# Six recurrence and output gate slabs in the seven-product scheme, with the operand sums kept through the branch projection and the first gates inside it

## The chip, the cores and the metric

The kernel runs on one core of one Trainium2 chip. The metric is the device time of one execution in microseconds (us), median over runs: 917.94 us for the kernel before (3 runs, 917.94 to 918.06). The profile below is of one further execution.

## The reference

One hybrid decoder block over 16 meta tokens and 512 tokens (T = 528), D = 1024, all in float32. Cut to what matters here:

```python
u = rmsnorm(h, mix_norm_w)
proj = u @ w_in                      # 1024 x 8192
q, k, v, g_ret, lru_in, lru_gate, gate_a, gate_b = split(proj)   # 1024 columns each
...                                  # rotary, chunked retention -> o
y_ret = (silu(g_ret) * o) @ w_branch_ret
c = causal_depthwise_conv(lru_in, conv_w, conv_b)                # 4 taps
r = sigmoid(c @ wa + ba);  i = sigmoid(c @ wx + bx)              # 4 blocks of 256 x 256
a = exp(-8 * r * softplus(-lam))
hs = scan(h -> a_t * h + sqrt(1 - a_t**2) * (i * c)_t)           # linear recurrence over time
y_lru = (gelu(lru_gate) * hs) @ w_branch_lru
h = h + (sigmoid(gate_a) * y_ret + sigmoid(gate_b) * y_lru) @ w_out
u = rmsnorm(h, ffn_norm_w)
g, up = split(u @ w_ffn_in)          # 2 x 2816 columns
h = h + (silu(g) * up) @ w_ffn_out
return rmsnorm(h, final_norm_w)[16:]
```

## The kernel before

Activations lie transposed, channels on the 128 partitions and time along the free axis. Every float32 product is made of three matmuls on rounded halves: an operand is stored as `hi` (a cast on ScalarE, line 291) and `lo` (source minus `hi`, a subtraction on VectorE, line 295), and `block` (lines 363 to 375 with `mm3`) issues hi·hi, hi·lo and lo·hi into one PSUM bank.

The weights `w_in` come as 32 **slabs** of 1024 x 256, four for each of the eight parts of `proj`: 16 to 19 are `lru_in`, 20 to 23 `lru_gate`, 24 to 27 `gate_a`, 28 to 31 `gate_b`. `w_fi` has 22 slabs of the same shape. A slab is four quarters `a11`, `a12`, `a21`, `a22` of 128 x 512, each against the matching quarters `b11` ... `b22` of the operand. A **plain** slab makes eight products of quarters (`plain`, 96 matmuls, 256 wide). A **fast** slab (`fast`, `fast512`, `fast528`) makes seven by the Strassen-Winograd scheme (84 matmuls). It needs sums of the weight quarters `s1` to `s4` (line 261, VectorE), sums of the operand quarters `t1` to `t4` (made once), and recombination: `ws` and `pz` (two copies on ScalarE, one add on VectorE, line 394) after the first two products, `u2` (a copy on ScalarE) after the last, and two adds on VectorE (lines 408 and 409) which read the two PSUM banks and so set them free. The product with `s4` goes into the bank that `pz` is read from, so it stands behind `pz`.

`PLAN` is the order of the mixing half: R (retention projections), A (`gate_a`), I (`lru_in` and its convolution), BR (`w_br`, the branch projection of retention, in two halves of eight k steps), T (the gates of one recurrence block, 48 matmuls of 264, each 6 followed by a sigmoid on ScalarE from PSUM), L (`lru_gate`, followed by gelu), B (`gate_b`, followed by tanh) and BL (`w_bl`). After BR stand `T0 L0 I2 T1 L1 I3 L2 T2 B0 L3 T3 B1 B2 B3 BL`. In that part all of L, I2, I3 and B are plain. The operand sums of `w_in` (t1 to t4) are freed ahead of BR.

`conv` (lines 1072 to 1086) is on VectorE: per half a block one tensor_scalar, three scalar_tensor_tensor, and the split into hi and lo. `recurrence` (lines 1113 to 1156) runs per block as a deferred generator, advanced while matmuls are issued: GpSimd multiplies `g*c` (line 1120, 1056 wide), ScalarE makes exp, tanh and sqrt, VectorE five scalar_tensor_tensor for each half, GpSimd `g1*t` (line 1146, 528 wide), VectorE a scan (line 1148), and at the end the product with the gelu (line 1153). ScalarE loads a function table when the function changes (sigmoid, exp/tanh, sqrt, gelu).

A timeline-driven scheduler puts the instructions of each engine in their final order when the program is built. On the chip each engine then takes its instructions in that order, and a consumer waits by semaphore. PSUM has eight banks, handed out in turn, so the first matmul into a bank waits for the reader that frees it. `pz`, `ws` and `u2` have one buffer each.

After BL come `w_out`, the residual, `out_norm` (norm factors, transposes with a diagonal matrix made on GpSimd for tiles 2 and 3), and the FFN: slabs 0 to 2 of `w_fi` are plain (slabs 0 and 1 by token halves), 3 to 21 fast, then `w_fo`.

Of the kernel before, what the change touches and what calls it, by code (L numbers as in the profile page):

```python
# [153 lines left out]
def hybrid_block(ctx: ExitStack, tc: tile.TileContext, a: dict):  # L154
# [60 lines left out]

    def plain_slab(key, i):
        if key == "w_in":
            return i in [{"Q": Q, "K": K, "G": G}[r[0]] + int(r[1]) for r in PLAIN_R] or LI + 2 <= i < GA or i >= GB
        return key == "w_fi" and i <= FIRST

    pieces = []
    for n, (key, i) in enumerate(order):
# [225 lines left out]
        plain("w_in", s, 256, [(pb[:, :256], pb[:, 256:]) for pb in pbs], UV)  # L448
        return pbs

    def branch(key, source, done):


        parts = {}
        for hf in range(2):
# [22 lines left out]
        nc.gpsimd.tensor_tensor(r[:parts, :w], v[:parts, :w], mhalf[:parts, :w], op=ALU.pow)  # L478
        return r[:parts, :w]

    def rms_factors(src, name, parts=P, diagonal=True):

        scratch = get(D)
        ssq = small.tile([P, 1], F32, tag="ssq", bufs=4, name=f"ssq_{name}")
        nc.scalar.activation(scratch[:parts], src, AF.Square, accum_out=ssq[:parts])
# [584 lines left out]
        convs[b] = defer(conv(b, xp, x3), 0.0)  # L1070

    def conv(b, xp, x3):
        c, ch, cl = get(2 * T), get(2 * T, F32R), get(2 * T, F32R)
        lru[b] = (c, ch, cl)
        c3, ch3, cl3 = (t.rearrange("p (j t) -> p j t", j=2) for t in (c, ch, cl))
        for j in range(2):
            k = 2 * b + j
            cw = [vec[:, V_CW + i * 8 + k:V_CW + i * 8 + k + 1] for i in range(4)]
            nc.vector.tensor_scalar(c3[:, j], x3[:, j], cw[3], vec[:, V_CB + k:V_CB + k + 1], ALU.mult, ALU.add)
            for i in range(1, 4):  # L1080
                nc.vector.scalar_tensor_tensor(c3[:, j, i:], x3[:, j, :T - i], cw[3 - i], c3[:, j, i:],
                                               ALU.mult, ALU.add)
# [31 lines left out]
    def recurrence(group):  # L1114
# [2 lines left out]

        A = {}
        for b, r, g, c in group:
            nc.gpsimd.tensor_tensor(g, g, c, op=ALU.mult)  # L1120
# [17 lines left out]
        for b, r, g, c in group:  # L1138
            for j in range(2):
                a, t, d, g1 = two(A[b])[:, j], two(r)[:, j], ds[b, j], two(g)[:, j]  # L1140
                nc.vector.scalar_tensor_tensor(d, a, 1.0, d, ALU.add, ALU.mult)
# [3 lines left out]
                nc.vector.scalar_tensor_tensor(t, a, 1.0, t, ALU.add, ALU.mult)
                nc.gpsimd.tensor_tensor(g1, g1, t, op=ALU.mult)
                yield STEPS[3]
                nc.vector.tensor_tensor_scan(t, a, g1, 0.0, ALU.mult, ALU.add)
# [4 lines left out]
            (nc.gpsimd if Z_POOL else nc.vector).tensor_tensor(z3, z3, two(r)[:, :, NM:], op=ALU.mult)
# [62 lines left out]

    def out_norm(t):
        if t >= 2:
            diag = held = rms_factors(h_sb[t], f"h{t}")
            rows = h_sb[t]  # L1220
        else:
            diag, rows = None, get(D)
            held = rows
            nc.vector.tensor_scalar_mul(rows, h_sb[t], rms_factors(h_sb[t], f"h{t}", diagonal=False))
        yield NORM
        for c in range(2):
            pb = transposed(rows, diag, c, f"hT{t}_{c}")
# [213 lines left out]
```

## Time and profile before

| | |
|---|---|
| median of the runs | 917.94 us (917.94 to 918.06) |
| the profiled execution: time, span | 918.17 us, 916.4 us |
| granted TensorE clock, mean | 0.997 |
| from 285.3 us: BR | 54.70 us |
| 340.0 to 472.2 us: L, I2, I3, T, B | 132.20 us |
| 472.2 to 516.5 us: BL | 44.30 us |
| 516.5 to 564.6 us: `w_out`, norm | 48.10 us |
| 564.6 to 600 us: `w_fi` slabs 0 to 2 | 35.40 us |
| 600 to 786 us: 19 fast slabs of `w_fi` | 186.00 us |

PE is TensorE, DVE is VectorE, ACT is ScalarE, POOL is GpSimd. A row of a group gives the line, the engine, the operation, the names, the shapes and the count, then busy time and mean ns of one. Instructions that follow one another on an engine overlap at their ends by some hundredth of a us, so a mean is longer than the pitch at which they follow.

### The profile page before, as it was taken

What the parts mean: (1) busy time and instruction counts of PE and PEld (TensorE: products, weight loads), DVE (VectorE), ACT (ScalarE), POOL (GpSimd) and SP (SyncE); (2) the same over time, 40 slices, a digit from 0 to 9 for tenths busy, and PEclk for the clock granted to TensorE, in tenths of its full rate; (3) what the DMA queues carried; (4) which work ended last, traced back from release to release, by engine and by line L of the source; (5) the groups of instructions that cost most, each with busy time, mean ns of one, the idle gap of its engine ahead of it and who ended that gap; (6) DMA issues with size and microseconds to landing.
All of it is one profiled execution on the core that took longest, in us unless ns stands there. A gap on an engine that the chain in (4) does not pass through costs nothing.

```text
span 916.4 us, 16814 instructions
## 1 busy us (share of the span) xinstructions
PE 904.4 (99%) x6572; PEld 854.1 (93%) x6572; DVE 657.7 (72%) x1082; ACT 463.2 (51%) x815; POOL 71.4 (8%) x81
## 2 busy tenths in 40 slices
PE   8999999999999999999999999999999999999996
PEld 7999999999999889999998889999999999888885
DVE  5988978986888738768735428878999998832223
ACT  6654546553556256757733315545555556632213
POOL 3000010000100011211200211000000000000003
PEclk9999999999999999999999999999999999999998
DMA  9323132231134332233342223223333333432202
GB/s 332 106 93 105 34 110 77 92 106 43 62 94 138 108 100 82 79 107 123 119 136 92 95 70 104 81 83 104 102 118 104 103 118 107 144 107 92 81 1 92
DMA packets 49071, 92.59 MB, mean 101 GB/s; under 512 B 5584, under 2 KB 5840, under 8 KB 48992
## 3 DMA queue, kind: packets, MB, share of 16 engines
q1 hardware_dynamic: 47408, 87.55, 29.4%
q10 hardware_dynamic: 1584, 3.97, 1.3%
q8 instruction: 51, 0.84, 0.4%
q14 instruction: 28, 0.23, 0.1%
HBM read 89.40 MB, written 2.10 MB: 100 GB/s over the span
## 4 chain that ended last, share of the span: by engine, by line
PE 79%; DVE 0%; issue 0%; POOLq 0%; POOL 0%; ACT 0%
PE fo L363 4%; PE fo L365 4%; PE fo L364 4%; PE zwf L375 4%; PE zwf L373 4%; PE zwf L374 4%; PE yxf L374 3%; PE yxf L375 3%; PE yxf L373 3%; PE gate L373 2%; PE lg L373 2%; PE lg L375 2%; PE gate L375 2%; PE gate L374 2%; PE lg L374 2%; PE wo L363 2%
## 5 line engine op out<-in xcount | busy, mean ns | idle before, releaser
L291 ACT CAST hi<-raw_w_in 128x512 fp32r<-128x512 f32 x99 | 61.0, 620 | 65.0 <-PE w_br L364 13.9
L295 DVE TENSOR_TENSOR lo<-raw_w_in,hi 128x512 fp32r<-128x512 f32 x99 | 70.4, 718 | 29.8 <-ACT hi L291 29.6
L375 PE MATMUL zwf<-b,lo 128*128 128x256 f32 x304 | 84.9, 279 | 0.0
L374 PE MATMUL zwf<-b,hi 128*128 128x256 f32 x304 | 84.9, 279 | 0.0
L373 PE MATMUL zwf<-b,hi 128*128 128x256 f32 x304 | 84.6, 279 | 0.0
L295 DVE TENSOR_TENSOR lo<-raw_w_fo,hi 128x512 fp32r<-128x512 f32 x44 | 30.1, 689 | 63.0 <-ACT hi L291 63.0
L291 ACT CAST hi<-s_w_fi 128x512 fp32r<-128x512 f32 x76 | 47.2, 622 | 45.5 <-PE zwf L374 36.3
L363 PE MATMUL fo<-hi,b 128*128 128x512 f32 x176 | 69.5, 395 | 0.0
L365 PE MATMUL fo<-hi,b 128*128 128x512 f32 x176 | 69.3, 394 | 0.0
L364 PE MATMUL fo<-lo,b 128*128 128x512 f32 x176 | 69.1, 392 | 0.0
L374 PE MATMUL yxf<-b,hi 128*128 128x256 f32 x228 | 63.2, 280 | 0.0
L375 PE MATMUL yxf<-b,lo 128*128 128x256 f32 x228 | 63.0, 279 | 0.0
L291 ACT CAST hi<-raw_w_fo 128x512 fp32r<-128x512 f32 x44 | 27.3, 621 | 69.8 <-PE fo L365 64.2
L291 ACT CAST hi<-raw_w_fi 128x512 fp32r<-128x512 f32 x69 | 42.3, 622 | 39.1 <-PE yxf L374 17.4
L373 PE MATMUL yxf<-b,hi 128*128 128x256 f32 x228 | 61.2, 279 | 0.0
L295 DVE TENSOR_TENSOR lo<-s_w_fi,hi 128x512 fp32r<-128x512 f32 x76 | 52.0, 687 | 12.2 <-ACT hi L291 10.4
L375 PEld LDWEIGHTS zwf<-b,lo 128*128 128x128 f32 x304 | 57.2, 188 | 0.0
L374 PEld LDWEIGHTS zwf<-b,hi 128*128 128x128 f32 x304 | 57.1, 188 | 0.0
L373 PEld LDWEIGHTS zwf<-b,hi 128*128 128x128 f32 x304 | 57.1, 188 | 0.0
L291 ACT CAST hi<-s_w_in 128x512 fp32r<-128x512 f32 x52 | 32.3, 620 | 40.4 <-PE zwgate L374 9.2
L295 DVE TENSOR_TENSOR lo<-raw_w_fi,hi 128x512 fp32r<-128x512 f32 x69 | 47.0, 687 | 6.0 <-ACT hi L291 5.9
L295 DVE TENSOR_TENSOR lo<-s_w_in,hi 128x512 fp32r<-128x512 f32 x52 | 35.5, 687 | 11.3 <-ACT hi L291 11.1
(422 smaller groups left out, 3134.0 us busy)
## 6 DMA issues: line engine op xcount, KB each, us to landing
raw_w_in<-in_w_in SPq DMA_DIRECT2D x112, 256.0 KB, 3.1
raw_w_fi<-in_w_fi SPq DMA_DIRECT2D x88, 256.0 KB, 3.2
raw_w_fo<-in_w_fo SPq DMA_DIRECT2D x44, 256.0 KB, 3.0
raw_w_br<-in_w_br SPq DMA_DIRECT2D x16, 256.0 KB, 3.1
raw_w_bl<-in_w_bl SPq DMA_DIRECT2D x16, 256.0 KB, 3.1
raw_w_out<-in_w_out SPq DMA_DIRECT2D x16, 256.0 KB, 2.9
raw_w_v<-in_w_v SPq DMA_DIRECT2D x15, 256.0 KB, 3.5
b<-in_x SPq DMA_DIRECT2D x4, 512.0 KB, 6.8
```

The lines of the kernel that those rows point to most:

```text
L291: nc.scalar.copy(hi, src)
L295: engine.tensor_tensor(lo, src, hi.bitcast(F32), op=ALU.subtract)
L363: nc.tensor.matmul(out, wh, xh, start=start, stop=False, skip_group_check=True)
L364: nc.tensor.matmul(out, wh, xl, start=False, stop=False, skip_group_check=True)
L365: nc.tensor.matmul(out, wl, xh, start=False, stop=stop, skip_group_check=True)
L373: nc.tensor.matmul(out, wh, xh, start=start and i == 0, stop=False, skip_group_check=True)
L374: nc.tensor.matmul(out, wh, xl, start=False, stop=False, skip_group_check=True)
L375: nc.tensor.matmul(out, wl, xh, start=False, stop=i == 3, skip_group_check=True)
```

## The change

- L0 to L3 (slabs 20 to 23), B0 and B3 (28 and 31) and slab 2 of `w_fi` are fast; I2, I3, B1 and B2 stay plain.
- The operand sums t1 to t4 are kept until BL.
- T0 leaves the plan and is issued inside the second half of BR, at its fifth k step; the splits of convolution blocks 0 and 1 are made there too, at the third and seventh.
- GpSimd's products `g*c` and `g1*t` of the recurrence are on VectorE.
- In a fast L slab the gelu is one instruction of 1024 from SBUF behind both adds, where two of 512 read PSUM.
- In `out_norm` ScalarE makes the diagonal for tiles 2 and 3, and the last tile waits 3.7 us where it waited 2.0.

```diff
-PLAN = "R0 R1 R2 R3 A0 A1 A2 A3 I0 I1 BR T0 L0 I2 T1 L1 I3 L2 T2 B0 L3 T3 B1 B2 B3 BL"
+PLAN = "R0 R1 R2 R3 A0 A1 A2 A3 I0 I1 BR L0 I2 T1 L1 I3 L2 T2 B0 L3 T3 B1 B2 B3 BL"
+PLAIN_L = "I2 I3 B1 B2".split()
+GATES_AT = 4
-NORM = 2.0
+NORM, LAST_NORM = 2.0, 3.7
...
-            return i in [{"Q": Q, "K": K, "G": G}[r[0]] + int(r[1]) for r in PLAIN_R] or LI + 2 <= i < GA or i >= GB
-        return key == "w_fi" and i <= FIRST
+            return i in [{"Q": Q, "K": K, "G": G, "I": LI, "L": LG, "B": GB}[r[0]] + int(r[1]) for r in PLAIN_R + PLAIN_L]
+        return key == "w_fi" and i < FIRST
...
+            if (key, i) == ("w_br", 1):
+                pieces[GATES_AT - KT:GATES_AT - KT] = [("gates", 0, c) for c in range(2)]
...
-    def branch(key, source, done):
+    def branch(key, source, done, between=lambda hf, k: None):
...
             for k in range(KT):
+                between(hf, k)
...
+        if by_scalar:
+            nc.scalar.activation(diag, ident, AF.Copy, scale=r)
+        else:
+            state["diag"] = nc.gpsimd.tensor_scalar_mul(diag[:parts, :parts], ident[:parts, :parts], r)
...
-            split((ch3[:, j], cl3[:, j]), c3[:, j], engine=nc.gpsimd if j in C_POOL else nc.vector)
-            yield CONV
+            if b > 1:
+                conv_parts(b, j)
+                yield CONV
...
+    def gates_between(hf, k):
+        if hf == 1 and k == GATES_AT - 2:
+            finish(convs[0])
+            conv_parts(0, 0)
+            conv_parts(0, 1)
+        elif hf == 1 and k == GATES_AT:
+            lru_gates(0)
+        elif hf == 1 and k == GATES_AT + 2:
+            finish(convs[1])
+            conv_parts(1, 0)
+            conv_parts(1, 1)
...
-            nc.gpsimd.tensor_tensor(g, g, c, op=ALU.mult)
+            nc.vector.tensor_tensor(g, g, c, op=ALU.mult)
...
-                nc.gpsimd.tensor_tensor(g1, g1, t, op=ALU.mult)
+                nc.vector.tensor_tensor(g1, g1, t, op=ALU.mult)
...
-        for j, pb in enumerate(plain512(LG + s, "lg")):
-            lookup(x[:, j * SEQ:(j + 1) * SEQ], pb, AF.Gelu_apprx_tanh)
+        if plain_slab("w_in", LG + s):
+            for j, pb in enumerate(plain512(LG + s, "lg")):
+                lookup(x[:, j * SEQ:(j + 1) * SEQ], pb, AF.Gelu_apprx_tanh)
+        else:
+            fast512("w_in", LG + s, UV, x, "lg")
+            lookup(x, x, AF.Gelu_apprx_tanh)
...
-            for b in ("t1", "t2", "t3", "t4"):
-                put(*U.pop(b))
-            branch("w_br", lambda i: R[i], gated(macc, GA))
+            branch("w_br", lambda i: R[i], gated(macc, GA), gates_between)
         elif step == "BL":
-            for b in ("b11", "b12", "b21", "b22"):
+            for b in list(U):
                 put(*U.pop(b))
...
-            diag = held = rms_factors(h_sb[t], f"h{t}")
+            diag = held = rms_factors(h_sb[t], f"h{t}", by_scalar=True)
...
-        yield NORM
+        yield NORM if t < NC_ - 1 else LAST_NORM
...
-    pbs = [bank(f"f{FIRST}_{q}") for q in range(2)]
-    plain("w_fi", FIRST, 256, [(pb[:, :256], pb[:, 256:]) for pb in pbs], VV)
-    ffn_gate(FIRST, *pbs)
...
-    for j in range(FIRST + 1, NJ):
+    for j in range(FIRST, NJ):
```

In the changed program line numbers are shifted: 295 (the `lo` subtraction) is 298, 261 (weight sums) 264, 394 (`pz`) 397, 408 and 409 (the two adds) 411 and 412, 1081 (convolution taps) 1088, 1148 (scan) 1174, 1153 (product with the gelu) 1179, 321 (lookups and table loads) 324.

**DVE while L2 ends and T2 stands on PE.** Before, VectorE has there the convolution of block 3 (`b_5027`) and the subtractions `lo` for the weights to come:

```order
569 L1081 SCALAR_TENSOR_TENSOR b_5027<-b_4881,vec,b_5027 128x527
570 L1081 SCALAR_TENSOR_TENSOR b_5027<-b_4881,vec,b_5027 128x526
571 L295 TENSOR_TENSOR lo_5064<-raw_w_in_1_5061,hi_5063 128x512
572 L1081 SCALAR_TENSOR_TENSOR b_5027<-b_4881,vec,b_5027 128x525
573 L295 TENSOR_TENSOR lo_5096<-raw_w_in_2_5093,hi_5095 128x512
574 L423 TENSOR_TENSOR b_5029<-b_5027,b_5028 128x528
575 L295 TENSOR_TENSOR lo_5126<-raw_w_in_3_5123,hi_5125 128x512
```

In the changed program the same convolution (`b_5064`) stands among the `lo` of seven products, the weight sums of the slab after next (`s_w_in`) and the product with the gelu, ahead of the two adds of L2:

```order
606 L264 TENSOR_TENSOR s_w_in_5291<-raw_w_in_2_5289,raw_w_in_0_5283 128x512
607 L1088 SCALAR_TENSOR_TENSOR b_5064<-b_4920,vec,b_5064 128x527
608 L298 TENSOR_TENSOR lo_5172<-s_w_in_5096,hi_5171 128x512
609 L1088 SCALAR_TENSOR_TENSOR b_5064<-b_4920,vec,b_5064 128x525
610 L298 TENSOR_TENSOR lo_5188<-raw_w_in_1_5084,hi_5187 128x512
611 L1179 TENSOR_TENSOR b_4745<-b_4745,b_4664 128x1024
612 L298 TENSOR_TENSOR lo_5208<-s_w_in_5092,hi_5207 128x512
613 L1088 SCALAR_TENSOR_TENSOR b_5064<-b_4920,vec,b_5064 128x526
614 L298 TENSOR_TENSOR lo_5300<-s_w_in_5287,hi_5299 128x512
615 L264 TENSOR_TENSOR s_w_in_5293<-s_w_in_5287,raw_w_in_2_5289 128x512
616 L411 TENSOR_TENSOR b_5049<-yxlg_5051,pzlg_5053 128x2x256
617 L412 TENSOR_TENSOR b_5049<-zwlg_5050,u2lg_5054 128x512
```

The adds of rows 616 and 617, which free both banks of L2, are new; the `pz` of L2 is row 598, and between it and row 616 stand rows 599 to 615: six `lo`, three weight sums, five convolution instructions, two scans and the product.

**ACT at the same place.** Before, ScalarE has the gelu of L2 in two halves from PSUM, with casts between them, and then the sigmoids of T2 (`gt`):

```order
385 L291 CAST hi_5125<-raw_w_in_3_5123 128x512
386 L291 CAST hi_5157<-raw_w_in_0_5155 128x512
387 L321 ACTIVATE b_5015<-lg_1_5017 128x512
388 L321 ACT_TABLE_LOAD
389 L321 ACTIVATE b_5162<-gt_1_0_5163,vec 128x264
390 L321 ACTIVATE b_5162<-gt_1_264_5171,vec 128x264
```

Now the gelu is row 401, of 1024 columns of the tile `b_5049` that row 617 of VectorE completes, and the sigmoids stand behind it:

```order
399 L402 COPY u2lg_5054<-yxlg_5051 128x256
400 L425 CAST b_5078<-b_5064 128x528
401 L324 ACTIVATE b_5049<-b_5049 128x1024
402 L324 ACT_TABLE_LOAD
403 L324 ACTIVATE b_5212<-gt_1_0_5213,vec 128x264
404 L324 ACTIVATE b_5212<-gt_1_264_5221,vec 128x264
```

The first sigmoid of T2 has moved from behind a read of PSUM to behind an SBUF tile that VectorE makes.

**PE at the same place.** Before, L2's 96 matmuls stand in one piece, and T2's 48 (`gt`) behind them:

```order
2891 L373 MATMUL lg_1_5017<-b_119,hi_4848 128x256
2892 L374 MATMUL lg_1_5017<-b_120,hi_4848 128x256
2893 L375 MATMUL lg_1_5017<-b_119,lo_4849 128x256
2894 L363 MATMUL gt_1_0_5163<-b_4653,hi_4919 128x264
2895 L364 MATMUL gt_1_0_5163<-b_4654,hi_4919 128x264
```

Now L2 stands in two parts: 48 matmuls (s1, s3, a12, a11) from row 2774, then 27 of T2, then from row 2849 the other 36 of L2, then T2's last 21, and B0 from row 2906:

```order
2847 L367 MATMUL gt_0_0_5245<-b_4687,hi_5013 128x264
2848 L368 MATMUL gt_0_0_5245<-b_4686,lo_5014 128x264
2849 L376 MATMUL yxlg_5051<-b_674,hi_4983 128x256
2850 L377 MATMUL yxlg_5051<-b_675,hi_4983 128x256
2851 L378 MATMUL yxlg_5051<-b_674,lo_4984 128x256
```

The last 12 of T2 (rows 2894 to 2905, tiles `gt_0_0_5261` and `gt_0_264_5269`) go into the banks that rows 616 and 617 of VectorE free; B0's first matmul goes into the bank that ACT's row 403 frees. B0 (48 in front, then 36) and L3 interleave in the same way, with T3's 48 before, between and behind L3's last 36. T3's last 12 (rows 3110 to 3121) go into the banks of L3's adds (VectorE's rows 657 and 661), and B1 (row 3122) waits for the first sigmoid of T3, which stands on ScalarE behind the gelu of L3 (row 445) and a table load. The `pz` of B0 and of L3 are VectorE's rows 628 and 650.

More of the change, by code (lines that the diff above doesn't have):

```diff
@@ L57 @@
 Z_POOL = False
-C_POOL = ()
 STEPS = (2.0, 2.0, 1.0, 2.0)
@@ L479, in rsqrt_mean, with rms_factors @@
         return r[:parts, :w]
-    def rms_factors(src, name, parts=P, diagonal=True):
+    def rms_factors(src, name, parts=P, diagonal=True, by_scalar=False):
         scratch = get(D)
@@ L490, in rms_factors @@
         diag = get(P)
-        state["diag"] = nc.gpsimd.tensor_scalar_mul(diag[:parts, :parts], ident[:parts, :parts], r)
+        if by_scalar:
+            nc.scalar.activation(diag, ident, AF.Copy, scale=r)
+        else:
+            state["diag"] = nc.gpsimd.tensor_scalar_mul(diag[:parts, :parts], ident[:parts, :parts], r)
         return diag
@@ L1072, in conv @@
     def conv(b, xp, x3):
-        c, ch, cl = get(2 * T), get(2 * T, F32R), get(2 * T, F32R)
-        lru[b] = (c, ch, cl)
-        c3, ch3, cl3 = (t.rearrange("p (j t) -> p j t", j=2) for t in (c, ch, cl))
+        c = get(2 * T)
+        lru[b] = (c,)
+        c3 = c.rearrange("p (j t) -> p j t", j=2)
         for j in range(2):
@@ L1083, in conv, with conv_parts @@
             yield CONV
-            split((ch3[:, j], cl3[:, j]), c3[:, j], engine=nc.gpsimd if j in C_POOL else nc.vector)
-            yield CONV
+            if b > 1:
+                conv_parts(b, j)
+                yield CONV
         put(xp)
+    def conv_parts(b, j):
+        if len(lru[b]) == 1:
+            lru[b] += get(2 * T, F32R), get(2 * T, F32R)
+        c3, ch3, cl3 = (t.rearrange("p (j t) -> p j t", j=2) for t in lru[b])
+        split((ch3[:, j], cl3[:, j]), c3[:, j])
+    def gates_between(hf, k):
[9 more added lines that the diff above has]
+            conv_parts(1, 1)
     def lru_gates(*blocks):
```

## The prediction

> **What bounds the kernel now.** First the engine rows of the page: busy time, share of the span, instructions.
>
> ```profile
> PE 904.4 (99%) x6572; PEld 854.1 (93%) x6572; DVE 657.7 (72%) x1082; ACT 463.2 (51%) x815; POOL 71.4 (8%) x81
> ```
>
> Then everything that PE waited for in the whole span:
>
> ```profile
> PE warm L186 <- POOL ident masks.py:199: 2.9, 1, 2.9
> PE yxq L373 <- ACT pzq L395: 0.9, 1, 0.9
> PE v L363 <- ACT b L582: 0.4, 1, 0.4
> PE v L364 <- DVE lo L295: 0.3, 1, 0.3
> PE v L365 <- DVE b L587: 0.2, 1, 0.2
> ```
>
> That is 4.7 us, none of it in the tiles `gt`, `lg`, `gate`, `w_br`, `w_bl`, `f`. So PE is the bound, a matmul less is worth its pitch, and moving other work can gain nothing there: it can only cost. Next, busy times by stage (PE, PEld, DVE, ACT, POOL, clock): BR, then L to B, then the three plain `w_fi` slabs, then 19 fast ones; and two pieces, one plain L slab and one pair of gates.
>
> ```profile
> 285.30:340.00 54.70, 54.70 (x279) 46.35 (x278) 36.19 (x61) 20.69 (x36) 1.80 (x1) 1.00 0.34 109
> 340.00:472.20 132.20, 132.20 (x1105) 132.20 (x1105) 96.35 (x130) 88.16 (x142) 22.23 (x12) 1.00 0.34 108
> 564.60:600.00 35.40, 35.40 (x307) 35.40 (x306) 29.25 (x41) 16.54 (x25) 1.43 (x3) 1.00 0.31 101
> 600.00:786.00 186.00, 186.00 (x1578) 185.38 (x1577) 170.65 (x276) 111.56 (x212) 0.00 (x0) 1.00 0.35 111
> ```
> ```profile
> 339.94:351.34 11.40, 11.40 (x98) 11.40 (x97) 7.28 (x12) 10.91 (x15) 2.41 (x2) 1.00 0.26 82
> 363.08:368.95 5.87, 5.87 (x50) 5.87 (x49) 4.89 (x10) 5.29 (x11) 0.39 (x1) 1.00 0.28 89
> ```
>
> A plain slab is 96 matmuls in 11.40 us, 0.1187 us each; a gate matmul is 5.87 / 48 = 0.122. Fast slabs in the FFN keep PE fed, but with DVE busy 170.65 of 186 us, 9.0 us for each slab of 9.8. There the DVE has little else. In the L to B stage it has the convolution and the recurrence as well, 96.35 of 132.2 us already.
>
> **What the change removes.** Seven slabs lose 12 matmuls each: 84 x 0.1187 = **9.98 us**. The profiled execution took 918.17 us, 0.23 over the median; all sums go from it. If nothing waits: 908.2.
>
> **What it adds to the DVE.** A fast slab adds 3 `lo`, 4 sums, a `pz` and 2 adds. Rows for the pitch of each:
>
> ```profile
> 561.02 2.49 DVE L295 TENSOR_TENSOR lo<-raw_w_fi,hi 128x512 fp32r<-128x512 f32 x4
> ```
> ```profile
> L261 DVE TENSOR_TENSOR s_w_fi<-raw_w_fi,raw_w_fi 128x512 f32<-128x512 f32 x33 | 22.7, 689 | 0.6
> L408 DVE TENSOR_TENSOR b<-yxf,pzf 128x512 f32<-128x512 f32 x18 | 12.3, 683 | 0.0
> L394 DVE TENSOR_TENSOR pzf<-zwf,wsf 128x256 f32<-128x256 f32 x19 | 7.9, 416 | 0.0
> ```
> ```profile
> 388.87 1.26 DVE L1148 TENSOR_TENSOR_SCAN b<-b,b 128x528 f32<-128x528 f32 x1 [1.22 <-POOL b L1146]
> 390.05 0.66 DVE L295 TENSOR_TENSOR lo<-raw_gates,hi 128x512 fp32r<-128x512 f32 x1
> 390.63 1.22 DVE L1153 TENSOR_TENSOR b<-b,b 128x1024 f32<-128x1024 f32 x1
> 391.77 0.16 DVE L1069 COPY b<-li 128x8 f32<-128x8 f32 x1
> 400.88 0.76 DVE L1081 SCALAR_TENSOR_TENSOR b<-b,vec,b 128x525 f32<-128x525 f32 x1
> 401.56 0.68 DVE L295 TENSOR_TENSOR lo<-raw_w_in,hi 128x512 fp32r<-128x512 f32 x1
> 416.06 0.70 DVE L1141 SCALAR_TENSOR_TENSOR b<-b,b 128x528 f32<-128x528 f32 x1
> 416.68 0.70 DVE L1134 SCALAR_TENSOR_TENSOR b<-b,b 128x528 f32<-128x528 f32 x1
> ```
>
> Four `lo` in 2.49 us with 0.69 for one: pitch 0.60, the mean less 0.09. So sums and adds 0.60, `pz` 0.33. From start to start: scan 1.18, product of 1024 columns 1.14, convolution tap 0.68 (its first operation, a tensor_scalar, 0.46), 528-wide operation 0.62. POOL's multiplies before:
>
> ```profile
> L1146 POOL TENSOR_TENSOR b<-b,b 128x528 f32<-128x528 f32 x8 | 13.6, 1706 | 50.8 <-DVE b L1145 47.8 <-ACT b L1068 3.1
> L1120 POOL TENSOR_TENSOR b<-b,b 128x1056 f32<-128x1056 f32 x4 | 10.4, 2595 | 138.0 <-ACT b L321 138.0
> ```
>
> On the DVE they are not shown; the nearest widths give 0.62 and 1.17. The range runs from these to POOL's own 1.71 and 2.60; I take the DVE rows, since the DVE is the engine that will do them. They shorten the chain of one block by 1.4 and 1.1 us at a time, but put 8 x 0.62 + 4 x 1.17 = 9.6 us more on the DVE. And POOL's work disturbs the DVE: of three equal `lo`, those under the POOL rows take twice as long.
>
> ```profile
> 408.23 2.60 POOL L1120 TENSOR_TENSOR b<-b,b 128x1056 f32<-128x1056 f32 x1 [19.39 <-ACT b L321]
> 420.44 1.64 POOL L1146 TENSOR_TENSOR b<-b,b 128x528 f32<-128x528 f32 x1 [9.60 <-DVE b L1145]
> ```
> ```profile
> 410.08 1.29 DVE L295 TENSOR_TENSOR lo<-raw_gates,hi 128x512 fp32r<-128x512 f32 x1 [1.58 <-ACT hi L291]
> 415.46 0.69 DVE L295 TENSOR_TENSOR lo<-raw_gates,hi 128x512 fp32r<-128x512 f32 x1
> 421.30 1.33 DVE L295 TENSOR_TENSOR lo<-raw_w_in,hi 128x512 fp32r<-128x512 f32 x1 [0.41 <-ACT hi L291]
> ```
>
> So I use undisturbed pitches throughout. The Trainium skill has the same in "GPSIMD Engine Reference", its table of specifications: GpSimd's SBUF interfaces are shared with VectorE, and contend with VectorE instructions that have two SBUF inputs. By it a `lo` beside POOL's work would count 1.3 and not 0.60, and the sum below would be worse without that part of the change; the rows agree.
>
> **Where the DVE comes last.** ACT's durations:
>
> ```profile
> L321 ACT ACT_TABLE_LOAD x16 | 20.5, 1283 | 0.3
> L321 ACT ACTIVATE b<-gt,vec 128x264 f32<-128x264 f32 x25 | 10.5, 492 | 0.0
> L321 ACT ACTIVATE b<-b,spm 128x528 f32<-128x528 f32 x8 | 5.8, 730 | 0.0
> L291 ACT CAST hi<-raw_w_in 128x512 fp32r<-128x512 f32 x32 | 19.5, 618 | 10.4 <-PE li L374 7.8 <-PE lg L374 1.8 <-ACT hi L291 0.8
> L321 ACT ACTIVATE b<-b 128x1024 f32<-128x1024 f32 x6 | 6.4, 1061 | 0.2 <-DVE b L409 0.2
> ```
>
> With the overlap off: table load 1.28, sigmoid 0.37, exp or tanh 0.61, cast 0.52; gelu of 1024 columns 1.06. Now I walk the new order, with time 0 at the first matmul of L2, everything punctual until then: between the `pz` of L1 and of L2 the DVE has 20.8 us of such work, PE 21.6.
>
> 1. `pz` of L2 (DVE row 598) needs 24 matmuls (2.85) and a copy of 0.4, so it ends at 3.7. Rows 599 to 617 are 6 `lo` 3.6, 3 sums 1.8, convolution 3.2, 2 scans 2.4, product 1.1, 2 adds 1.2: 13.3. The adds end at 16.4 and 17.0. PE wants their banks for T2's last 12 matmuls at 84 x 0.1187 + 36 x 0.122 = 14.4 and 15.1. Loss so far 2.1.
> 2. The gelu of L2 stands ahead of T2's sigmoids: 17.0, gelu 1.06, table load 1.28, sigmoid 0.37, with the semaphores' time 19.95. B0's first matmul, due at 15.8, waits for that. Loss 4.1.
> 3. Behind it on ACT stand 7 more sigmoids, a table load, 2 exps, a tanh and 4 casts ahead of the copy `ws` of B0: 28.05. The DVE waits for these casts and exps (rows 622 to 627). `pz` of B0 (row 628) ends at 28.8; PE, due at 23.8, waits with B0's last 36. Loss 5.1.
> 4. Rows 629 to 650 are 9 `lo` 5.4, 8 recurrence operations 5.0, a GpSimd multiply moved here 0.6, scan 1.2, 2 adds 1.2, `pz` 0.3: 13.7, and some 1.1 of waits for ACT. `pz` of L3 ends at 43.6, due 37.3. Loss 6.3.
> 5. Rows 651 to 661: 3 `lo` 1.8, 3 sums 1.8, scan 1.2, multiply 0.6, product 1.1, 2 adds 1.2: 7.7. The last add of L3 ends at 51.35; T3's last 6 matmuls wanted its bank at 40.9. Loss 10.5.
> 6. Gelu of L3, table load, sigmoid of T3: 54.25. B1's first matmul was due at 41.6. **Loss 12.65.**
>
> Behind B1 the next fast slab is B3, two plain slabs later, with 30.3 us of DVE work against PE's 38.5: no more is lost, and none is won back, since PE has no slack.
>
> **The other parts, at nothing.** T0 and the splits in BR: 4 splits 2.5, 2 `lo` 1.2 and a recurrence of 12, some 16 us more on the DVE in a stage where it is busy 36.19 of 54.70, with PE 5.9 longer; bounds 0 to 1. `w_fi` slab 2: 5.7 us of DVE on 29.25 of 35.40, of which 4.2 (`lo`, sums) may be made earlier; bounds 0 to 2, when the operand sums come late. Diagonals on ACT and the last tile's later transposes: 1.7 us more matmuls stand between, ACT has half the stage free; 0 to 0.5. Kept sums: SBUF slots, no time. If the DVE enters step 1 late by the lag of earlier rounds (L0, L1), up to 2 more. Below nothing none can go: PE has no wait to give back.
>
> **Rivals.** *Nothing waits*: 908.2. For it: the FFN rows, where fast slabs cost no wait. Against: 9.0 of 9.8 us there without convolution or recurrence. *The DVE's work alone counts* and the round trips through ACT in steps 2 and 3 vanish: from `pz` of L2, 13.3 + 7.1 (rows 618 to 628) + 13.7 + 7.7 ends at 45.5, B1 then starts 2.9 later at 48.4, a loss of 6.8: 918.17 − 9.98 + 6.8 = 915.0. For it: a bank may turn over a little sooner. This is also the faster side's main mechanism, deciding as soon as the loss is under 10 us. *The clock drops too*. In the last 16 us PE works 9.18:
>
> ```profile
> 900.00:916.00 16.00, 9.18 (x40) 7.07 (x38) 4.83 (x7) 5.06 (x11) 4.98 (x10) 0.86 0.26 99
> ```
> ```profile
> 2.91 4.62 PE L186 MATMUL warm<-ident 128*128 128x128 f32 x22 [2.91 <-POOL ident masks.py:199]
> ```
>
> The granted clock is 0.86 there, so an idle PE loses it. A single wait of the walk is at most 2.2 us, but two of them (steps 5 and 6) stand 0.7 us apart. A restart as long as the warm-up row, 4.6 us at half rate, would cost 2.3: 923.1 once, 925.4 twice. The Trainium skill, "TensorE: Matmul & The Clock Gate", Part 1 on the HAM clock gate, speaks against the change here: the clock halves after an idle window of about 3.4 us. By that an estimate of 1.7 us for each such window stands in place of 2.3; that PE's waits of 2.9 us at the start show no lower clock agrees.
>
> **How the numbers follow.** The walk 0.5: 918.17 − 9.98 + 12.65 = **920.8**, and 919 to 923 with the bounds. Work alone 0.2: 915.0, 913 to 917. Nothing waits 0.2: 908.2 to 910.5. Clock 0.1: 923 to 925.5. The range of 8 in 10 runs from 908.5 to 925. A measurement tells some 0.2% (1.8 us) from no change. Slower, over 919.8: 0.36 of the walk and the clock's 0.1, 0.46. Within: 0.14 of the walk and 0.04 of work alone, 0.18. Faster: 0.36.
>
> **What would show it.** PE's waits: `gt`, `gate` and `zwlg` released by DVE adds and `pz` and by ACT sigmoids, some 13 us in all between L2 and B1, none before `w_br` ends or in the FFN. If those waits sum to under 3 us, the first rival holds; if PE's granted clock is under 1.00 in these 55 us, the last. Waits of `f` tiles at the FFN's start would show its operand sums late. The walk is wrong if DVE pitches are not those of before, or if `pz` of L2 is not where the lag begins.

## The result and the profile after

The changed kernel takes **927.13 us** (median of 4 runs, 925.96 to 927.55) against 918.0 us for the one before in the same session (4 runs, 917.94 to 918.29): ratio 1.0093, 95% interval 1.0081 to 1.0104. It is slower by about 9 us. The forecast was 920.8, with 908.5 to 925.0 as the range: the side was right, the size too small by 6 us.

The profiled execution took 927.3 us, its span is 925.5 us. The engine row of its page, and after it all that PE waited for from the recurrence gates on (the rows of the first 200 us are left out):

```profile
PE 902.2 (97%) x6488; PEld 849.6 (92%) x6488; DVE 696.1 (75%) x1164; ACT 482.0 (52%) x853; POOL 45.1 (5%) x67
```
```profile
PE gt L366 <- DVE b L411: 6.2, 2, 4.6
...
PE gt L366 <- DVE b L412: 1.9, 1, 1.9
PE gate L376 <- ACT b L324: 1.5, 1, 1.5
...
PE zwgate L376 <- DVE pzgate L397: 0.5, 1, 0.5
PE zwgate L376 <- ACT b L324: 0.5, 1, 0.5
...
PE zwlg L376 <- DVE pzlg L397: 0.2, 1, 0.2
```

Before, none of these tiles waited. Now T2 and T3 (`gt`) wait for the two adds of L2 and L3, B0 (`zwgate`) and B1 (`gate`) for sigmoids on ACT, and the second parts of B0 and L3 for `pz`: 10.8 us in all, the places that the prediction named.

The stages (busy time and count of PE, PEld, DVE, ACT, POOL, then the clock): L0 to L2, L2 to B1, and B1 to BL:

```profile
340.68:389.91 49.23, 49.23 (x409) 49.23 (x408) 48.67 (x83) 35.16 (x62) 0.00 (x0) 1.00 0.31 103
389.91:446.94 57.03, 46.06 (x350) 44.05 (x349) 49.55 (x78) 36.63 (x64) 0.00 (x0) 0.92 0.28 92
446.94:477.51 30.57, 30.57 (x241) 30.57 (x241) 22.95 (x31) 22.32 (x36) 0.00 (x0) 0.93 0.27 90
```

The second and third rows are longer than their matmuls at full rate. From the first matmul of L2 to that of B1 41.6 us were due; it took 57.03, **15.4 us** more, of which PE stood idle for 57.03 − 46.06 = 11.0. The other 4.4 are matmuls that took longer, and so are 2.1 us behind B1 (240 matmuls in 30.57 us, due 28.5). Both go with a granted clock of 0.92 and 0.93. The first row is the quiet part of the story: PE loses nothing from L0 to L2, but the DVE is busy 48.67 of 49.23 us there.

The clock in pieces of 2 us, around the two longest stretches of waiting (same columns):

```profile
404.00:406.00 2.00, 0.43 (x4) 0.22 (x2) 2.00 (x4) 0.96 (x3) 0.00 (x0) 1.00 0.22 64
406.00:408.00 2.00, 0.00 (x0) 0.00 (x0) 2.00 (x4) 0.00 (x0) 0.00 (x0) 0.74 0.34 109
408.00:410.00 2.00, 1.01 (x4) 1.02 (x5) 2.00 (x4) 0.44 (x1) 0.00 (x0) 0.50 0.00 0
410.00:412.00 2.00, 1.99 (x10) 1.68 (x8) 1.42 (x3) 1.98 (x3) 0.00 (x0) 0.50 0.00 0
...
414.00:416.00 2.00, 2.00 (x20) 2.00 (x18) 1.63 (x3) 2.00 (x5) 0.00 (x0) 1.00 0.00 0
...
444.00:446.00 2.00, 1.33 (x6) 1.03 (x6) 1.22 (x3) 1.95 (x2) 0.00 (x0) 0.63 0.52 159
446.00:448.00 2.00, 1.06 (x5) 1.06 (x6) 0.00 (x0) 1.99 (x6) 0.00 (x0) 0.50 0.32 103
448.00:450.00 2.00, 2.00 (x11) 2.00 (x11) 1.61 (x2) 2.00 (x5) 0.00 (x0) 0.50 0.03 8
```

The DVE is busy in every microsecond of 404 to 410, while PE stands from 404.43 to 408.99. The clock falls to 0.50, and the rows at 0.50 in which PE is busy throughout count 10 or 11 matmuls in 2 us, where the row at 1.00 counts 20.

How the DVE holds PE is read from its timeline at `pz` of L2 and at L2's adds (start, duration):

```profile
395.89 0.42 DVE L397 TENSOR_TENSOR pzlg<-zwlg,wslg 128x256 f32<-128x256 f32 x1
...
407.64 0.68 DVE L264 TENSOR_TENSOR s_w_in<-s_w_in,raw_w_in 128x512 f32<-128x512 f32 x1
408.25 0.68 DVE L411 TENSOR_TENSOR b<-yxlg,pzlg 128x512 f32<-128x512 f32 x1
408.85 0.68 DVE L412 TENSOR_TENSOR b<-zwlg,u2lg 128x512 f32<-128x512 f32 x1
```

From the start of `pz` to the end of the second add, 409.45, are 13.56 us without a gap; the walk had 13.28 + 0.33 = 13.6. But L2 began at 389.91, so `pz` started 5.98 us into it; the walk had 3.4. The DVE brought a lag of **2.6 us** into L2, and the wait of 2.1 became 4.6.

The lag is older than L2. The first matmul of L1, and L1's `pz`:

```profile
368.21 0.28 PE L376 MATMUL zwlg<-b,hi 128*128 128x256 f32 x1
```
```profile
374.90 0.42 DVE L397 TENSOR_TENSOR pzlg<-zwlg,wslg 128x256 f32<-128x256 f32 x1
```

L1's `pz` starts 6.69 us into L1, 3.3 later than the 3.4 of the walk, and L0's starts 8.8 us into L0 (349.49 − 340.68). PE lost nothing by it there, because matmuls of I2 and I3 stand between the two parts of L0 and of L1. From `pz` of L1 to `pz` of L2 are 20.99 us, and the prediction had counted 20.8 of DVE work. In the 4.68 us ahead of L0 the DVE was already busy for 4.60, with the recurrence of block 0, whose gates now stand inside BR, and with reads of the banks of `w_br`. Which of them brought the lag was not tested.

Behind the adds of L2 ACT does what step 2 said:

```profile
409.56 1.06 ACT L324 ACTIVATE b<-b 128x1024 f32<-128x1024 f32 x1 [4.60 <-DVE b L412]
410.62 1.28 ACT L324 ACT_TABLE_LOAD   x1
411.92 2.34 ACT L324 ACTIVATE b<-gt,vec 128x264 f32<-128x264 f32 x6
```

Here the last column names what ended ACT's idle time: 4.60 us, until the second add of L2. Gelu, table load, then T2's sigmoids. PE's timeline shows the matmuls that the walk named, with the wait in front of each:

```profile
408.99 0.59 PE L366 MATMUL gt<-b,hi 128*128 128x264 f32 x1 [4.56 <-DVE b L411]
```
```profile
412.45 0.58 PE L376 MATMUL zwgate<-b,hi 128*128 128x256 f32 x1 [0.46 <-ACT b L324]
```
```profile
421.72 0.39 PE L376 MATMUL zwgate<-b,hi 128*128 128x256 f32 x1 [0.47 <-DVE pzgate L397]
436.36 0.39 PE L376 MATMUL zwlg<-b,hi 128*128 128x256 f32 x1 [0.21 <-DVE pzlg L397]
444.07 0.39 PE L366 MATMUL gt<-b,hi 128*128 128x264 f32 x1 [1.95 <-DVE b L412]
446.94 0.58 PE L376 MATMUL gate<-b,hi 128*128 128x256 f32 x1 [1.53 <-ACT b L324]
```

Less 389.91 and the due times of the walk (14.4, 15.8, 23.8, 37.3, 40.9, 41.6) these give the loss at each step:

| step | walk | measured |
|---|---|---|
| 1, first bank of L2 | 2.1 | 4.7 |
| 2, B0 begins | 4.1 | 6.7 |
| 3, second part of B0 | 5.1 | 8.0 |
| 4, second part of L3 | 6.3 | 9.2 |
| 5, last bank of L3 | 10.5 | 13.3 |
| 6, B1 begins | 12.65 | 15.4 |

From step 1 on the two run in parallel, 2.6 to 2.9 us apart.

### The profile page after: what moved, and what is told of

Read it like the earlier page. It is cut to its first block, busy times and chain, and to the rows that moved or that the text cites. A ratio compares the mean times of both kernels' runs of the same rounds, so it can differ in the third digit from the quotient of the medians.

```text
span 925.5 us, 16780 instructions
## 1 busy us (share of the span) xinstructions
PE 902.2 (97%) x6488; PEld 849.6 (92%) x6488; DVE 696.1 (75%) x1164; ACT 482.0 (52%) x853; POOL 45.1 (5%) x67
## 4 chain that ended last, share of the span: by engine, by line
PE 75%; DVE 2%; ACT 1%; issue 1%; POOLq 0%; POOL 0%; DVEq 0%
PE fo L368 4%; PE fo L366 4%; PE fo L367 4%; PE zwf L376 4%; PE zwf L378 4%; PE zwf L377 4%; PE yxf L378 3%; PE yxf L376 3%; PE yxf L377 3%; PE wo L368 2%; PE w_bl L368 2%; PE wo L366 2%; PE wo L367 2%; PE w_bl L366 2%; PE w_br L367 2%; PE w_br L368 2%
## 5 line engine op out<-in xcount | busy, mean ns | idle before, releaser
L378 PE MATMUL zwf<-b,lo 128*128 128x256 f32 x320 | 89.6, 280 | 0.0
L376 PE MATMUL zwf<-b,hi 128*128 128x256 f32 x320 | 89.5, 280 | 0.0
L377 PE MATMUL zwf<-b,hi 128*128 128x256 f32 x320 | 89.4, 279 | 0.0
L294 ACT CAST hi<-raw_w_in 128x512 fp32r<-128x512 f32 x93 | 57.3, 619 | 50.6 <-PE zwlg L377 6.8
L294 ACT CAST hi<-s_w_in 128x512 fp32r<-128x512 f32 x76 | 47.0, 621 | 56.1 <-PE zwgate L377 9.0
L298 DVE TENSOR_TENSOR lo<-raw_w_in,hi 128x512 fp32r<-128x512 f32 x93 | 62.9, 682 | 16.4 <-ACT hi L294 16.2
L377 PE MATMUL yxf<-b,hi 128*128 128x256 f32 x240 | 66.3, 280 | 0.0
L378 PE MATMUL yxf<-b,lo 128*128 128x256 f32 x240 | 66.3, 280 | 0.0
L376 PE MATMUL yxf<-b,hi 128*128 128x256 f32 x240 | 64.1, 280 | 0.0
L298 DVE TENSOR_TENSOR lo<-s_w_in,hi 128x512 fp32r<-128x512 f32 x76 | 51.8, 685 | 13.7 <-ACT hi L294 13.4
L376 PEld LDWEIGHTS zwf<-b,hi 128*128 128x128 f32 x320 | 60.3, 188 | 0.0
L378 PEld LDWEIGHTS zwf<-b,lo 128*128 128x128 f32 x320 | 60.2, 188 | 0.0
L377 PEld LDWEIGHTS zwf<-b,hi 128*128 128x128 f32 x320 | 60.1, 188 | 0.0
```

Of the source, the lines that this page charges most:

```text
L294: nc.scalar.copy(hi, src)
L298: engine.tensor_tensor(lo, src, hi.bitcast(F32), op=ALU.subtract)
L376: nc.tensor.matmul(out, wh, xh, start=start and i == 0, stop=False, skip_group_check=True)
L377: nc.tensor.matmul(out, wh, xl, start=False, stop=False, skip_group_check=True)
L378: nc.tensor.matmul(out, wl, xh, start=False, stop=i == 3, skip_group_check=True)
```

## The experiments

Theory 1 is the prediction's: six fast slabs fill the DVE between L0 and B1, its queue holds the adds and `pz`, and PE waits for them. Its supplement after the result: the clock falls as well, and the lag begins before L2. The rivals are told with each run. All times are medians of three executions or more, except where a single one is named; waits are those of the one execution that was traced; ratios are to the kernel before on the same chip (918.4 to 918.6 us).

**All six plain, the rest of the change kept.**

```diff
-PLAIN_L = "I2 I3 B1 B2".split()
+PLAIN_L = "L0 L1 L2 L3 I2 I3 B0 B1 B2 B3".split()
```

> L0 to L3, B0 and B3 plain again; all other parts of the change stay (first gates inside the branch projection, POOL multiplies on VectorE, diagonals on ACT, w_fi slab 2 fast). Theory 1 (the six fast slabs fill VectorE between the first L slab and B1, and this alone makes the loss): no wait between L2 and B1 over 0.5 us, granted clock 1.00 there, time 918.0 - 1.4 = 916.6, 916 to 918. Rival 2 (the other edits, above all the multiplies moved to VectorE, make part of the loss): over 919, with waits of gt or gate tiles.

Measured: 918.1 us, ratio 0.9996 (0.9987 to 1.0006). PE waits nowhere after the first 200 us. So T0 in the branch projection, the multiplies on VectorE, the diagonals on ACT and slab 2 of `w_fi` cost no wait; rival 2 falls. Of the 1.4 us that slab 2 should save 0.4 is seen, and the time lies 0.1 above the expected 916 to 918. About half of the 1.4 is missing in the FFN itself: from the first matmul of `w_fi` to that of `w_fo` are 217.3 us in this trace and 218.0 before. No wait is listed there, and the cause stays open.

**B0 plain.**

```diff
-PLAIN_L = "I2 I3 B1 B2".split()
+PLAIN_L = "I2 I3 B0 B1 B2".split()
```

> B0 plain, the other six slabs fast: PE has 1.4 us more, VectorE 5.7 us less between L2 and T3. Theory 1: the first wait of T2 falls from 4.6 to about 3, later ones by as much as VectorE lost, the sum of waits from 12 to 4 to 7 us and one clock drop goes: 918 to 921. Rival 3 (the round trips through ACT, gelu and table load ahead of the sigmoids, hold PE whatever VectorE has to do): waits stay near 10 us, 925 or more.

Measured: 920.78 us, ratio 1.003 (1.0017 to 1.0043). PE's waits in its trace:

```profile
PE gate L376 <- ACT b L324: 3.6, 2, 1.9
...
PE gt L366 <- DVE b L411: 1.5, 2, 0.9
...
PE gt L366 <- DVE b L412: 0.8, 1, 0.8
```

Less work for the DVE shortens the waits for its adds from 8.1 us to 2.3. T2's first wait falls to 0.6 us, below the 3 that were expected, although the DVE is as busy from L0 to L2 (48.66 of 49.22 us): its order moved, and from the start of L2's `pz` to that of the first add are 6.3 us (404.22 − 397.92) where the change has 12.4. The waits for sigmoids behind the gelu grow from 2.0 us to 3.6, so rival 3 holds for these two places, and not for the sum. The traced execution was a long one, of 922.76 us.

**PE kept busy in its waits.**

```diff
+HOLD = {(4, 0, 264): 34, (6, 0, 264): 16}
...
-                            i == 0, i == 1)
+                            i == 0, i == 1 and not hold(k, which, sl.start))
+                    for n in range(hold(k, which, sl.start)):
+                        nc.tensor.matmul(pb, zeros, ch3[:, 0, sl], start=False, stop=n == hold(k, which, sl.start) - 1,
+                                         skip_group_check=True)
...
+    def hold(k, which, start):
+        return HOLD.get((k, which, start), 0)
```

`zeros` holds zero weights, so the sums stay as they are. There are 34 such matmuls in the tile of T2 that stands ahead of the waits for L2's banks, and 16 in T3's.

> The changed kernel, with 34 matmuls of 264 with zero weights added to T2's tile ahead of the two waits for L2's banks, and 16 to T3's ahead of the waits for L3's banks: PE is busy for 4.1 and 2.0 us in which it would have waited, the result and VectorE's work stay. Theory 4 (the granted clock falls because PE stands idle there, and costs about 5 us on top of the waits): clock 1.00 from L2 to B1 or one drop left, waits down by about 5, time 922 to 924.5. Rival 5 (the clock falls for another reason, or costs nothing, since PE waits there anyway): 926 to 928.

Measured: 924.09 us, ratio 1.0065 (1.0049 to 1.0082): 50 matmuls more, and 0.28% or 2.6 us less than the changed kernel. Windows of its trace, L2 to B1 and B1 to BL:

```profile
389.38:444.03 54.65, 48.62 (x400) 47.78 (x398) 49.55 (x79) 36.92 (x65) 0.00 (x0) 1.00 0.30 96
444.03:474.15 30.12, 30.12 (x241) 30.12 (x242) 22.84 (x31) 21.81 (x35) 0.00 (x0) 0.94 0.29 91
```

The clock is 1.00 from L2 to B1, with the same 49.55 us of DVE work, and the stage takes 54.65 us, 2.4 less than 57.03. The drop at B1 is still there (0.94). So the clock fell because PE stood idle, as theory 4 has it. What the drop at T2 costs is not the whole 2.4 us, though. B0 begins with this matmul:

```profile
411.92 0.39 PE L381 MATMUL zwgate<-b,hi 128*128 128x256 f32 x1 [1.74 <-ACT b L329]
```

That is 22.54 us into L2, exactly as in the changed kernel (412.45 − 389.91): up to there the drop cost nothing, because PE had to wait for the sigmoid anyway, 1.74 us here and 0.46 there. B0's first six matmuls then take 0.8 us where they took 1.4. Behind them the order of the instructions on the DVE and ACT is no longer that of the changed kernel, so the rest of the 2.4 can't be put down to the clock.

**The plain slabs B1 and B2 moved between the fast ones.**

```diff
-PLAN = "R0 R1 R2 R3 A0 A1 A2 A3 I0 I1 BR L0 I2 T1 L1 I3 L2 T2 B0 L3 T3 B1 B2 B3 BL"
+PLAN = "R0 R1 R2 R3 A0 A1 A2 A3 I0 I1 BR L0 I2 T1 B1 L1 I3 L2 T2 B2 B0 L3 T3 B3 BL"
```

> The changed kernel with the plain slabs B1 and B2 moved between the fast ones: L0 I2 T1 B1 L1 I3 L2 T2 B2 B0 L3 T3 B3 BL; the same work on every engine. Theory 1 (VectorE's peak between L0 and B1 is what costs, not its total): the two plain slabs give it 22.8 us of PE time with 4.8 us of its own work, most waits go, 909 to 914. Rival 6 (the whole stage is too full for VectorE, or the coupling at gelu and T3 holds in any order): 918 or more.

Measured: 931.2 us, ratio 1.0138 (1.0123 to 1.0153), worse than the change. PE's longest waits:

```profile
PE w_bl L366 <- ACT b L425: 8.6, 1, 8.6
PE zwgate L376 <- ACT b L324: 3.0, 1, 3.0
```

The expectation missed, and the time is on rival 6's side (918 or more). The waits from T2 to B3 are shorter than with the change, 7.5 us where they were 10.8. But B1 and B2 behind T3 had covered the recurrence of block 3; with B3 alone there BL waits 8.6 us for its operand. They are no spare time that can be put elsewhere.

**Three fast slabs: L0, L1 and B3 (and slab 2 of `w_fi`).**

```diff
-PLAIN_L = "I2 I3 B1 B2".split()
+PLAIN_L = "L2 L3 I2 I3 B0 B1 B2".split()
```

> L0, L1, B3 and w_fi slab 2 fast, L2, L3 and B0 plain. Theory 1 (waits come from VectorE's backlog when fast slabs stand beside T2 and T3): L0 and L1 cost nothing, as in the changed kernel; no wait over 0.5 us, clock 1.00, 3 slabs less work than with none of the six fast (918.1): 918.1 - 3 x 1.4 = 913.8, 913 to 915. Rival 3 (waits at T2 and T3 stay as long as any slab before them is fast): 917 or more.

Measured: 913.57 us, ratio 0.9947 (0.993 to 0.9963), faster than both. No wait of PE after the first 200 us, and from 340 us on:

```profile
340.00:470.00 130.00, 130.00 (x1078) 129.53 (x1077) 108.30 (x166) 90.61 (x151) 0.00 (x0) 1.00 0.35 112
```

**Four: L2 fast as well.**

```diff
-PLAIN_L = "I2 I3 B1 B2".split()
+PLAIN_L = "L3 I2 I3 B0 B1 B2".split()
```

> As the last, with L2 fast too: PE 1.4 us less; L2's adds stand again in front of T2. Theory 1: the waits at T2 of the kernel with B0 plain alone stay, about 3.7 us, those at T3 (3.0 and a clock drop) go: 912.4 + 3.7 = 916, 915 to 917.5. Rival: L2 is harmless when B0 and L3 are plain, 912.5.

Measured: 916.37 us, ratio 0.9984 (0.9974 to 0.9993). The waits at T2 are back, 1.9 us for L2's first add and 1.7 for the sigmoid ahead of B0: one fast slab in the wrong place takes its 1.4 us and 2.8 more. Its ten executions fall into two groups: six of 916.1 to 916.4 and four of 918.2 to 918.6. The profiled one, 918.62, shows why:

```profile
406.00:408.00 2.00, 1.55 (x12) 1.32 (x11) 0.96 (x2) 1.62 (x2) 0.00 (x0) 0.84 0.47 165
408.00:410.00 2.00, 0.73 (x3) 0.73 (x4) 0.00 (x0) 1.99 (x5) 0.00 (x0) 0.50 0.01 4
410.00:412.00 2.00, 2.00 (x11) 2.00 (x10) 1.27 (x2) 2.00 (x6) 0.00 (x0) 0.50 0.00 0
```

PE waited from 403.93 to 405.80, had 12 matmuls until 407.55, and waited again until 409.27. The clock fell at 407.38, so ahead of the second wait: one wait of 1.9 us stands before the drop. The mean clock of the six shorter executions is 0.996 to 0.998, of the four longer ones 0.994 or less. So the drop comes in some executions and not in others; that the waits are the same in both is likely, but only a longer one was traced.

**The gelu behind the sigmoids.**

```diff
+GELU = 5.4
...
-            lookup(x, x, AF.Gelu_apprx_tanh)
+            def gelu():
+                lookup(x, x, AF.Gelu_apprx_tanh)
+                Z[s] = x
+                return
+                yield
+
+            defer(gelu(), GELU)
+            return
         Z[s] = x
```

> The changed kernel with the gelu of a fast L slab issued behind the sigmoids of the gates that follow. Steps 2 and 6 of the prediction (gelu and two table loads ahead of the first sigmoid hold B0 and B1) are worth at most 2 x 2.3 us; theory 1: VectorE's backlog holds PE at the banks as before and the 4.6 us wait and the clock drop stay: 922 to 925. Rival 3 (the round trip through ACT is the main cost): 919 or less.

Measured: 922.43 us, ratio 1.0046 (1.0031 to 1.0061), 0.47% or 4.3 us less than the change.

```profile
PE gt L367 <- DVE b L413: 2.6, 1, 2.6
PE gt L367 <- ACT b L325: 2.4, 1, 2.4
PE gate L377 <- ACT b L325: 2.3, 1, 2.3
PE gt L367 <- DVE b L412: 1.5, 2, 1.1
```

The time is within the expected 922 to 925, but not for the expected reason. The wait of 4.6 us and the clock drop at T2 did not stay: T2's only wait is the 2.4 us for ACT, and the clock is 1.00 there. B0's wait is gone. B1 still waits 2.3 us, and the 2.6 us are T3's, for the second add of L3. The whole order moved, so the 4.3 us are what the run as a whole gives, and not the price of steps 2 and 6 alone.

**The multiplies back on GpSimd.**

```diff
-            nc.vector.tensor_tensor(g, g, c, op=ALU.mult)
+            nc.gpsimd.tensor_tensor(g, g, c, op=ALU.mult)
...
-                nc.vector.tensor_tensor(g1, g1, t, op=ALU.mult)
+                nc.gpsimd.tensor_tensor(g1, g1, t, op=ALU.mult)
```

> The changed kernel with the recurrence's multiplies on GpSimd again: 9.6 us less for VectorE, but lo beside them took 1.3 where alone 0.69, and the chains get 1.1 to 1.4 us longer each time. Theory 7 (a multiply on GpSimd costs VectorE about as much as doing it): 925 to 929. Rival 8 (the moved multiplies are what fills VectorE): waits 5 us shorter, 920 to 923.

Measured: 930.29 us (median of 929.35, 930.29 and 930.89), ratio 1.0126 (1.011 to 1.0143). A fourth execution, the traced one, took 3053 us and is left out. The waits come from another execution of the same kernel:

> The changed kernel with the recurrence's multiplies on GpSimd again, for its waits: theory 7, waits at T2 and T3 as long as in the changed kernel or longer and lo of up to 1.3 us beside GpSimd's multiplies; time 929 to 931 as timed before.

929.93 us, with 12.6 us of waits of `gt`, `gate`, `zwgate` and `zwlg`. One operation of the DVE and the one of GpSimd that runs at the same time, then GpSimd's group from 340 to 480 us:

```profile
430.28 1.83 DVE L1167 SCALAR_TENSOR_TENSOR b<-b,b 128x528 f32<-128x528 f32 x1
429.93 1.61 POOL L1172 TENSOR_TENSOR b<-b,b 128x528 f32<-128x528 f32 x1 [11.71 <-ACT wslg L396]
```
```profile
L1172 POOL TENSOR_TENSOR b<-b,b 128x528 f32<-128x528 f32 x8 | 17.2, 2148 | 72.4 <-DVE b L1171 60.7 <-ACT wslg L396 11.7
```

Rival 8 falls. Each engine disturbs the other: a `scalar_tensor_tensor` of 0.70 us takes 1.83, and GpSimd's multiply 2.15 us on average where it took 1.71 in the kernel before. That part of the change is worth 3 us.

**L1 plain.**

```diff
-PLAIN_L = "I2 I3 B1 B2".split()
+PLAIN_L = "L1 I2 I3 B1 B2".split()
```

> The changed kernel with L1 plain: VectorE has 5.7 us less ahead of L2, so that pz of L2 should come punctually, as step 1 of the prediction assumed. Theory 10 (the walk was right from a punctual start, and the lag of 2.6 us that VectorE brought into L2 and the clock drop it caused were what it lacked): first wait of T2 about 2.1, no clock drop there, B1's start 12 to 13 us behind its due time at most, or 2.5 more with a drop at T3: 921 to 925. Rival 11 (the lag arises at L2 itself): first wait over 4, 927 or more.

Measured: 922.12 us, ratio 1.0041 (1.0027 to 1.0055). PE's waits:

```profile
PE gate L376 <- ACT b L324: 2.4, 1, 2.4
PE gt L366 <- DVE b L411: 2.3, 2, 1.2
PE zwgate L376 <- ACT b L324: 1.7, 1, 1.7
...
PE gt L366 <- DVE b L412: 1.4, 1, 1.4
```
```profile
390.82:441.57 50.75, 42.86 (x351) 41.81 (x349) 43.79 (x72) 37.00 (x63) 0.00 (x0) 0.98 0.33 104
```

L1 has 1.4 us of matmuls more, and still the time is 5.0 us less: L2 to B1 takes 50.75 us where it took 57.03. The second add of L2 starts 15.5 us into L2 (406.36 − 390.82), with the change 18.9, in the walk 16.4. T2's first wait is 1.2 us, and the clock falls only at T3. So rival 11 falls, and theory 10, that the walk lacked the backlog of L0 and L1, fits. The run does not isolate it, though: B1 begins 9.2 us late (50.75 − 41.6), earlier than the 12.65 of a walk from a punctual start, because 5.8 us of DVE work have left the stretch from L2 to B1 as well (43.79 against 49.55). One thing was expected wrongly: `pz` of L2 does not come earlier but 7.0 us into L2. The order gives the freed time to the work behind `pz`, so lag has to be counted in work done by the adds, not at `pz`.

**Four fast: L0, L1, B2 and B3.**

```diff
-PLAIN_L = "I2 I3 B1 B2".split()
+PLAIN_L = "L2 L3 I2 I3 B0 B1".split()
```

> L0, L1, B2, B3 and w_fi slab 2 fast; L2, L3, B0, B1 plain: the kernel with three fast slabs and one more, behind the last pair of gates. Theory 1: between B1 and the branch projection VectorE was busy 22.95 of 30.57 us in the changed kernel; a fast B2 adds 5.7, which fits, so 1.4 less than with three: 912.2, 911.5 to 913. Rival 9 (the recurrence of block 3 gets late for the branch projection): 914 or more, with a wait of w_bl.

Measured: **912.19 us**, ratio 0.9934 (0.9919 to 0.9948), no wait of PE after the first 200 us: the fastest of all. The time is the expected one, and rival 9 falls.

**Six fast, elsewhere.**

```diff
-PLAIN_L = "I2 I3 B1 B2".split()
+PLAIN_L = "L2 L3 I2 I3".split()
```

> Six fast slabs as in the changed kernel, but L0, L1, B0, B1, B2 and B3; L2 and L3 plain. The same number of matmuls and of VectorE instructions as the changed kernel. Theory 1, sharpened (not the number of fast slabs costs but that the adds and the gelu of L2 and L3 stand ahead of T2's and T3's sigmoids, and that VectorE has the recurrence of blocks 1 to 3 at the same time): no wait over 0.5 us and two slabs less work than with four fast (912.2): 912.2 - 2 x 1.4 = 909.4, 908.5 to 911. Rival 12 (VectorE cannot carry six fast slabs in this stage wherever they stand): waits of gate or w_bl tiles, 914 or more.

Measured: 912.95 us, ratio 0.9939 (0.9923 to 0.9956). As many matmuls as the change, and 14 us less. PE's waits for `pz` and its copy are short, but 2.3 us together, and two slabs more than in the last kernel bring nothing where they should bring 2.8:

```profile
PE zwgate L376 <- DVE pzgate L397: 1.7, 2, 1.1
...
PE yxgate L376 <- ACT pzgate L398: 0.6, 1, 0.6
```

Neither side of the expectation holds: the place of the fast slabs counts far more than their number, but the fifth and the sixth gain nothing here. Their waits are for `pz`; the time is 3.6 us from 912.19 − 2.8, and the waits explain 2.3 of it. Five fast slabs and other places for six were not tried.

## Why the prediction was right or wrong

- *PE is the bound, and 84 matmuls are worth 9.98 us*: right. With places that cost no wait, 3 slabs took 4.5 us off the kernel with none (913.57 against 918.1).
- *The DVE becomes the bound from L2 to B1*: right, place and mechanism. T2, T3, B0, B1 and the second parts wait for the adds, `pz` and sigmoids named, and 11.0 us of idle PE stand against 12.65 in the walk.
- *Step 1, everything punctual until then*: **wrong**, and this is the largest part of what the size lacks. It rested on 20.8 us of DVE work against 21.6 of PE between the `pz` of L1 and of L2. Both figures were right (20.99 and 21.70 measured), but they say only that the lag does not grow there, not that there is none. The DVE was 3.3 us late at L1's `pz` already and 2.6 at L2's, and B1 begins 15.4 us late where the walk had 12.65: 2.8 us. The prediction named this sign of being wrong itself ("if `pz` of L2 is not where the lag begins"), and it held a lag of up to 2 us for a bound, but put it at nothing in the sum.
- *The clock as a rival of its own, at 1 in 10*: **wrong as placed**. It is no alternative to the walk, but comes on top of it: waits as short as the walk's 2.1 us can bring the drop, as the single wait of 1.9 us ahead of it in the kernel with four fast slabs shows. The price of 2.3 us a time was about right where PE waits for nothing else: behind B1 the slow matmuls cost 2.1, and the two groups of executions with four fast slabs lie 2.1 apart. At T2 most of it fell into a wait that was there anyway. That the waits at the start show no lower clock supports nothing: the 22 warm-up matmuls behind them took between 4.19 us (all six plain) and 4.96 (three fast), so their rate was not always the same.
- *The sum*: 920.8, plus 2.8 of lag, plus 2.1 of slow matmuls behind B1, is 925.7; the profiled execution took 927.3. The other 1.6 us lie outside the walk: L0 begins 0.7 us later than before, of which PE's waits in the first stage (`v`, 1.4 us against 0.9) are a part, a stage that the change leaves as it was; and from the first matmul of `w_fi` to that of `w_fo` slab 2 saves 0.6 us (217.4 against 218.0) and not 1.4.
- *Steps 2 to 6*: right; behind step 1 each adds what the walk gave it, to within 0.3 us. With the gelu behind the sigmoids the kernel is 4.3 us faster, but its order moved as a whole, so what steps 2 and 6 cost by themselves stays open.
- *Multiplies on VectorE at undisturbed pitch*: right, 930 us with them on GpSimd.
- *T0, diagonals, `w_fi` slab 2 at nothing*: no wait, 918.1 us by themselves; but slab 2's own 1.4 us is seen only in part, and whether the recurrence of block 0, which T0's place moves ahead of L0, brought the lag was not tested.

## What to carry to other kernels

When a change takes work from the bound engine and gives it to one that is busy three quarters of the time, add up the second engine's work stretch by stretch from the first stretch on, and carry its lag along; 99% busy without a wait is a warning, not a proof of cover. Then look at what stands behind its late instructions on a third engine, and price the waits with the clock that they cost. How many slabs are converted matters less than where: four places that do not stand directly in front of T2 and T3 gave 0.66%; six with L2 and L3 among them cost 0.93%, and six without these two gave 0.61%.

## What had not been expected of the hardware

A wait need not be long to lower the granted clock: in the kernel with four fast slabs and L2 among them, one wait of 1.9 us with 12 matmuls behind it was followed by the drop; by their clocks four executions of ten had it. In the changed kernel the clock fell at 406.98, 2.55 us after PE went idle, and stayed at 0.50 for 6.8 us, the last 4.8 of them with PE back at work. In the 3.4 us ahead of the falls PE was busy for 0.86 us there, for 1.45 at T3, and for 1.58 in the kernel with four fast slabs. The Trainium skill, "TensorE: Matmul & The Clock Gate", Part 1, has one idle window of about 3.4 us for the fall, and says of the window that it runs freely. That the same program falls into two groups, 2.1 us apart, agrees with a freely running window; the short waits, with PE busy for up to 1.58 of the 3.4 us, do not agree with a window that has to be idle throughout.
